# A second DMA queue on ScalarE, shared places for the memory pieces, and refitted engine choices in a two-block transformer kernel

## The chip, the cores and the metric

One core of a Trainium2 chip runs the whole program. The core has a TensorE (PE in the profile, with its weight loads as PEld), a VectorE (DVE), a ScalarE (ACT), a GpSimd (POOL) and a SyncE (SP), each of which takes its own instructions strictly in order, and 16 DMA engines. A transfer is started by an instruction on one of the engines. That instruction waits, like any other, until what it needs is there, and whatever stands behind it on its engine waits with it. The metric is device time in microseconds (us), the median of several runs.

## The reference

All arrays are fp32, with 256 tokens of width 1024. The first block mixes tokens in two ways (block attention over 8 heads, and differential attention over 4 heads, both with a relative position bias), attends to a memory, and ends with a SwiGLU. The second block has an RWKV-7 layer and a latent-attention (MLA) layer with a SwiGLU each. Cut to what matters here:

```python
# first block
h = rms_norm(x, mix_norm_g)
qa, ka, va, qb, kb, vb = split(h @ w_in)
oa = moba_attention(qa, ka, va, rel_bias_table[:, :8])     # logits + bias[bucket(t - s)], softmax
ob = diff_attention(qb, kb, vb, rel_bias_table[:, 8:], lam)
x = x + concat(oa, ob) @ w_out
x = x + memory_cross_attention(x, mem)                     # keys and values from rms_norm(mem)
x = x + (silu(g @ w_gate) * (g @ w_up)) @ w_down           # g = rms_norm(x)
x = rms_norm(x, final_norm_g)
# second block: RWKV-7 layer, whose state S follows, token by token and head by head,
S = S * w[t] + (S @ a[t]) b[t]^T + v[t] k[t]^T ;  y[t] = S @ r[t]
# ... then group norm, a bonus from r * k * r_k, a gate, memory attention, w_out, SwiGLU;
# MLA layer with rope, memory attention, w_out, SwiGLU;
return rms_norm(x, final_norm_g)
```

## The kernel before

Every weight product is done in three passes, since each fp32 operand is split into a high and a low part: `ah` and `al` are the parts of an activation, `wh` and `wl` those of a weight, and `acc` receives `ah*wh + ah*wl + al*wh`. Weights come in panels of 512 KB (two blocks of 128 rows by 512 columns). `panel` loads a panel into `wr` by a DMA issued on SP; there are three such buffers. A CAST on ScalarE or VectorE makes `wh`, and a subtraction on VectorE makes `wl`. TensorE uses them in `gemm`.

Everything is recorded first as a list of operations from many generators, and then put in order for each engine. The class `Order` does this: `link` finds the dependences and `play` runs a list scheduler over them with a table of costs. DMAs have a cost of issuing and of starting (`DMA_ISSUE`, `DMA_START`) and one clock `dma` of the bytes moved; `RUSH` adds an offset to the priority of each kind of operation. `LEAN` shifts which engine takes an operation that several can do, and `SIDE` names operations that go to VectorE instead of the default GpSimd (or the other way round). The result is a fixed order for each engine, found before the program runs. All instructions are emitted from one line (L2730), so a row is told by its tiles.

The places that matter here:

- **Start.** `setup` makes constants, one tiny ScalarE ACTIVATE (`warm`), and a few matmuls on zeros. The gains (all norm vectors in one tile, `gains`) and the input (`xres`, four pieces of 256 KB) are loaded by SP, between the first weight panels.
- **Bias** (`rel_bias`). The bucket table times a one-hot matrix gives a vector, which goes to memory (`relonce`), is copied there into 24 rows (`rel`), and is read back skewed as the tile `bias` (128 x 256 x 12, 1.5 MB, two DMAs). VectorE adds it to the scores (`e<-pst,bias`).
- **Memory** (`project_mem`). The memory's 8 blocks come in four pieces (`memt`); both blocks' memories go through it, the second's under the name `mem_2t`.
- **Inverses** (`inverses`). The RWKV-7 layer is computed in chunks, each with a triangular inverse. Its matrices `m271h` and `m271l` (first half of the tokens; `m272h` and `m272l` the second) go to memory as `d_m`, come back as 96 rows (`kk<-d_m`), and 31 steps of forward substitution run on GpSimd (first half, `kk`, `subtmp`) or VectorE (second half, `tm`). The result goes out as `d_x` and back as `xt<-d_x`. VectorE masks `xt` (`xt<-xt,m`), and TensorE merges blocks of it (`ident,xt`, then `ymerge` and `x` products).
- **Semaphores.** Each DMA counts on one of eight counters (`DMAHW0` to `DMAHW7`), taken in turn in program order over all issuing engines. A DMA also waits for the counter's earlier DMA.

## Time and profile before

| what | value |
|---|---|
| median of 3 runs | 1139.57 us (1138.84 to 1144.2) |
| profiled execution, its own time | 1143.02 us |
| span of the profiled execution | 1141.3 us |
| mean granted TensorE clock | 0.986 |
| busy share PE, DVE, ACT, POOL | 97%, 75%, 38%, 15% |
| DMA | 183.27 MB, mean 161 GB/s |

The busy share is busy time over span. A clock of 1.00 is 2.4 GHz; a stretch at 1.2 GHz shows as 0.50, and matmuls there take longer without TensorE being idle, so the loss of a stretch has two parts: idle time, and busy time at the lower level. The idle time in brackets at the end of a row is what the engine stood still before that row, with the instruction or transfer that ended it.

### The profile page before, as it was taken

To read this page: it belongs to the slowest core of one execution; us is meant where nothing else is said; L and a number is where in the kernel's file an instruction comes from. 1 tells how busy PE (TensorE), PEld (TensorE's weight loads), DVE (VectorE), ACT (ScalarE), POOL (GpSimd) and SP (SyncE) were. 2 spreads that over 40 slices of the span, in tenths; PEclk is the share of its full clock that TensorE was granted. 3 is DMA by queue.
4 is the path that set the end of the run, shared out by engine and by line. 5 is a ranking of instruction groups with operands and counts; after the bars stand their busy time and mean duration, and the time that the engine had idled before them with its cause. 6 is when DMAs were issued, how large, how long until landed. Compare 5 with 4: busy or idle time off the path is not lost.

```text
span 1141.3 us, 21650 instructions
## 1 busy us (share of the span) xinstructions
PE 1110.4 (97%) x8716; PEld 1052.6 (92%) x8716; DVE 854.8 (75%) x1454; ACT 429.5 (38%) x857; POOL 171.3 (15%) x199
## 2 busy tenths in 40 slices
PE   8899999999999999899979999999999999999997
PEld 7798999999999999799768999999999889999985
DVE  7658577677776777979787877766878968777584
ACT  5437442545223214635323532223235765212400
POOL 1200101024111013016601121120012002111100
PEclk9999999999999999899989999999999999999999
DMA  8744355266564655347320355556654425555563
GB/s 260 231 153 145 120 176 181 86 193 208 168 208 140 214 187 180 121 117 215 102 65 14 96 182 180 176 163 186 195 169 140 153 95 170 184 185 179 175 207 105
DMA packets 116164, 183.27 MB, mean 161 GB/s; under 512 B 19175, under 2 KB 41480, under 8 KB 116040
## 3 DMA queue, kind: packets, MB, share of 16 engines
q1 hardware_dynamic: 115920, 181.37, 51.8%
q8 instruction: 68, 1.11, 0.4%
q0 software_dynamic: 144, 0.52, 0.2%
q14 instruction: 32, 0.26, 0.1%
HBM read 178.84 MB, written 3.48 MB: 160 GB/s over the span
## 4 chain that ended last, share of the span: by engine, by line
PE 84%; DVE 8%; DMA 4%; ACT 2%; issue 1%; SPq 0%; POOLq 0%; POOL 0%; ACTq 0%; DVEq 0%
PE acc L2730 73%; PE pst L2730 11%; DVE wl L2730 3%; DMA wr<-in_w_in_dram 1%; DVE e L2730 1%; ACT wh L2730 1%; DMA wr<-in_a_ffn_down_dram 1%; DVE tm L2730 1%; DVE qt L2730 0%; DMA wr<-in_b_w_out_dram 0%; DMA wr<-in_w_down_dram 0%; ACT e L2730 0%; DVE wh L2730 0%; DMA xres<-in_x_t_dram 0%; DMA wr<-in_a_ffn_gu_dram 0%
## 5 line engine op out<-in xcount | busy, mean ns | idle before, releaser
L2730 DVE TENSOR_TENSOR wl<-wr,wh 128x1024 fp32r<-128x1024 f32 (+3 forms) x358 | 411.4, 1157 | 107.5 <-ACT wh L2730 93.9
L2730 PE MATMUL acc<-ah,wh 128*128 128x256 f32 x2224 | 482.9, 283 | 4.6 <-ACT ah L2730 2.3
L2730 PE MATMUL acc<-ah,wl 128*128 128x256 f32 x2224 | 481.4, 284 | 2.0 <-DVE wl L2730 1.7
L2730 PE MATMUL acc<-al,wh 128*128 128x256 f32 x2224 | 481.6, 283 | 0.4 <-DVE al L2730 0.4
L2730 PEld LDWEIGHTS acc<-ah,wh 128*128 128x128 f32 x2224 | 357.9, 189 | 10.1 <-ACT ah L2730 3.6
L2730 PEld LDWEIGHTS acc<-ah,wl 128*128 128x128 f32 x2224 | 357.3, 189 | 5.7 <-DVE wl L2730 3.4
L2730 PEld LDWEIGHTS acc<-al,wh 128*128 128x128 f32 x2224 | 357.6, 189 | 2.7 <-DVE al L2730 1.3
L2730 ACT CAST wh<-wr 128x1024 fp32r<-128x1024 f32 (+4 forms) x199 | 181.3, 915 | 371.0 <-PE acc L2730 284.0
L2730 DVE CAST wh<-wr 128x1024 fp32r<-128x1024 f32 (+2 forms) x159 | 115.2, 726 | 68.1 <-PE acc L2730 46.8
L2730 POOL TENSOR_TENSOR h<-h,bc 128x512 f32<-128x512 f32 x33 | 51.6, 1568 | 267.9 <-ACT h L2730 267.7
L2730 PE MATMUL acc<-wh,ah 128*128 128x512 f32 (+2 forms) x212 | 66.2, 372 | 2.6 <-ACT wh L2730 2.4
L2730 PE MATMUL acc<-wl,ah 128*128 128x512 f32 (+2 forms) x212 | 66.1, 370 | 0.7 <-DVE wl L2730 0.5
L2730 PE MATMUL acc<-wh,al 128*128 128x512 f32 (+2 forms) x212 | 66.7, 373 | 0.0
L2730 POOL TENSOR_TENSOR tm<-tm 128x512 f32<-128x512 f32 (+1 forms) x18 | 27.4, 1525 | 222.3 <-ACT tm L2730 188.3
L2730 PEld LDWEIGHTS acc<-wh,ah 128*128 128x128 f32 x212 | 39.8, 193 | 9.4 <-ACT wh L2730 3.2
L2730 PEld LDWEIGHTS acc<-wl,ah 128*128 128x128 f32 x212 | 39.9, 192 | 7.9 <-DVE wl L2730 1.3
L2730 PEld LDWEIGHTS acc<-wh,al 128*128 128x128 f32 x212 | 39.8, 192 | 7.0 <-issue 0.3
L2730 ACT ACTIVATE h<-h 128x512 f32<-128x512 f32 x33 | 20.4, 629 | 62.3 <-DVE h L2730 62.1
L2730 ACT CAST ah<-h 128x512 fp32r<-128x512 f32 x32 | 19.7, 621 | 39.4 <-DVE h L2730 39.2
L2730 ACT ACTIVATE ah<-xres,gains 128x256 fp32r<-128x256 f32 x55 | 24.9, 500 | 16.4 <-DVE xres L2730 14.9
L2730 DVE TENSOR_TENSOR xres<-acc,xres 128x512 f32<-128x512 f32 x24 | 16.3, 687 | 18.9 <-PE acc L2730 18.8
L2730 DVE SCALAR_TENSOR_TENSOR al<-xres,gains,ah 128x256 fp32r<-128x256 f32 x56 | 28.6, 542 | 1.0 <-ACT ah L2730 0.9
(350 smaller groups left out, 1027.6 us busy)
## 6 DMA issues: line engine op xcount, KB each, us to landing
wr<-in_a_ffn_gu_dram SPq DMA_DIRECT2D x40, 512.0 KB, 3.8
wr<-in_b_ffn_gu_dram SPq DMA_DIRECT2D x40, 512.0 KB, 3.9
wr<-in_w_in_dram SPq DMA_DIRECT2D x22, 512.0 KB, 4.6
wr<-in_w_down_dram SPq DMA_DIRECT2D x22, 512.0 KB, 4.6
wr<-in_a_ffn_down_dram SPq DMA_DIRECT2D x22, 512.0 KB, 4.5
wr<-in_b_ffn_down_dram SPq DMA_DIRECT2D x22, 512.0 KB, 3.8
wr<-in_w_gate_dram SPq DMA_DIRECT2D x20, 512.0 KB, 4.3
wr<-in_w_up_dram SPq DMA_DIRECT2D x20, 512.0 KB, 4.0
```

Source lines behind the costliest of these rows:

```text
L2730: emit(*map(again, x.args), **{k: again(v) for k, v in x.kw.items()})
```

## The change

It does four things. 27 DMAs that SP issued are issued by ScalarE: the gains, the four pieces of the input, the one-hot matrix and the table, `relonce`, `rel` and both parts of `bias`, and all transfers of the inverses. In the planner each issuing engine gets a DMA clock of its own. The pieces of both memories come from one pool under shared names, so that the second memory's pieces take the places of the first's. And the tables that set order and engines (`RUSH`, one entry of `LEAN`, `SIDE`) are new. In `SIDE`, `last` and `sq` are dropped (two additions of the output and of the squares go to GpSimd), and `rls`, `ms` and `rk` are added (the scaling of mean squares and the product of r and k go to VectorE). In `setup`, gains and input are now ahead of the `warm` ACTIVATE.

```diff
-    DMA_ISSUE = {"sync": 450.0, "gpsimd": 1000.0}
-    DMA_START = {"sync": 1100.0, "gpsimd": 1900.0}
+    DMA_ISSUE = {"sync": 450.0, "scalar": 450.0, "gpsimd": 1000.0}
+    DMA_START = {"sync": 1100.0, "scalar": 1100.0, "gpsimd": 1900.0}
...
-        order, dma, table = [], 0.0, None
+        order, dma, table = [], dict.fromkeys(names, 0.0), None
...
-                dma = max(dma, ready[i]) + op.size / 360.0
-                free[e] = end = max(free[e] + self.DMA_ISSUE[e], dma + self.DMA_START[e])
+                dma[e] = max(dma[e], ready[i]) + op.size / 360.0
+                free[e] = end = max(free[e] + self.DMA_ISSUE[e], dma[e] + self.DMA_START[e])
...
-                dma = end = max(dma, start + self.DMA_START[e]) + op.size / (360.0 if start > self.DMA_COLD else 240.0)
+                end = max(dma[e], start + self.DMA_START[e]) + op.size / (360.0 if start > self.DMA_COLD else 240.0)
+                dma[e] = end
...
-RUSH = {'a_k1152.0': 21100, 'a_k768.0': -1000, ...
+RUSH = {'a_k1152.0': 12300, 'a_k768.0': 4400, ...
...
-LEAN = {... 'rope': 3462, ...
-SIDE = {'last': 'vector', 'gate': 'vector', 'kk': 'vector', 'rope': 'vector', 'sq': 'vector', 'x': 'vector'}
+LEAN = {... 'rope': 4671, ...
+SIDE = {'gate': 'vector', 'kk': 'vector', 'rls': 'vector', 'rope': 'vector', 'x': 'vector', 'ms': 'vector', 'rk': 'vector'}
...
+        self.x = cp.tile([128, 8, S], F32, name="xres")
+        self.load_gains()
         nc.scalar.activation(self.small(1, "warm", 1), self.neghalf[:, :1], AF.Square)
...
-        self.x = cp.tile([128, 8, S], F32, name="xres")
-        self.load_gains()
...
-        self.nc.sync.dma_start(gt, self.a["gains"])
+        self.nc.scalar.dma_start(gt, self.a["gains"])
...
+        self.turns.pop("memt", None)
...
-        nc.sync.dma_start(once, vec)
+        nc.scalar.dma_start(once, vec)
...
-        nc.sync.dma_start(rows, once.strided(0, [[0, m], [1, n]]))
+        nc.scalar.dma_start(rows, once.strided(0, [[0, m], [1, n]]))
...
-            nc.sync.dma_start(bias[:, j:j + 128].rearrange("p j h -> p (j h)"),
+            nc.scalar.dma_start(bias[:, j:j + 128].rearrange("p j h -> p (j h)"),
...
-            nc.sync.dma_start(self.x[:, b:b + 2],
+            nc.scalar.dma_start(self.x[:, b:b + 2],
...
-                t2 = self.go(self.later(norm, self.project_mem(pool, "mem", g["mem_norm_g"], memacts, mn, 2)), "mem")
+                t2 = self.go(self.later(norm, self.project_mem(self.memp, "mem", g["mem_norm_g"], memacts, mn, 2)), "mem")
...
-        self.t_mem = self.go(self.project_mem(self.memp, "mem_2", g["mem_norm_g_2"], self.memacts, self.mn, 1), "a_mem")
+        self.t_mem = self.go(self.project_mem(self.memp, "mem_2", g["mem_norm_g_2"], self.memacts, self.mn, 2), "a_mem")
...
-                nc.sync.dma_start(d_m[c][6 * i:6 * i + 6, :128].rearrange("u s t -> s u t"), self.mbs[c, i])
+                nc.scalar.dma_start(d_m[c][6 * i:6 * i + 6, :128].rearrange("u s t -> s u t"), self.mbs[c, i])
...
-                nc.sync.dma_start(ms[48 * i:48 * i + 48], d_m[c].strided(0, [[32 * 128 + 32, 48], [128, 32], [1, 32]]))
-            nc.sync.dma_start(xs, a["sub_start"])
+                nc.scalar.dma_start(ms[48 * i:48 * i + 48], d_m[c].strided(0, [[32 * 128 + 32, 48], [128, 32], [1, 32]]))
+            nc.scalar.dma_start(xs, a["sub_start"])
...
-                nc.sync.dma_start(self.d_x[c].strided(32 * i, [[1024, 48], [64, 16], [1, 32]]), xs[48 * i:48 * i + 48])
+                nc.scalar.dma_start(self.d_x[c].strided(32 * i, [[1024, 48], [64, 16], [1, 32]]), xs[48 * i:48 * i + 48])
...
-            nc.sync.dma_start(last, self.d_x[c].rearrange("u b s t -> (b s) u t"))
+            nc.scalar.dma_start(last, self.d_x[c].rearrange("u b s t -> (b s) u t"))
```

The orders show what this does on each engine. In them a number behind a name tells copies of a tile apart, and the bracket lists the semaphores on which a row waits.

ScalarE before, at the start of the program:

```order
L2730 ACT_TABLE_LOAD
L2730 ACTIVATE warm_92<-neghalf 128x1 [waits Pool_49]
L2730 CAST wh_70<-wr_69 128x512 [waits DMAHW0_49]
L2730 CAST wh_70<-wr_69 128x512 [waits DMAHW1_49]
L2730 CAST wh_73<-wr_72 128x512 [waits DMAHW2_49]
L2730 ACTIVATE ah_81<-xres,gains 128x256 [waits DMAHW4_49,DMAHW3_49]
```

ScalarE now, at the same place (there `DMAHW0` counts the gains, `DMAHW2` the first piece of the input, `DMAHW3` the second half panel of weights):

```order
L2732 DMA gains<-in_gains_dram 128x149
L2732 DMA xres<-in_x_t_dram 128x2x256 x3
L2732 DMA xres<-in_x_t_dram 128x2x256 [waits DMAHW0_49]
L2732 DMA onehot<-in_rel_onehot_dram 33x384 [waits DMAHW2_49]
L2732 DMA reltab<-in_rel_bias_table_dram 32x12 [waits DMAHW3_49,DVE_49]
L2732 ACT_TABLE_LOAD
L2732 ACTIVATE warm_92<-neghalf 128x1 [waits Pool_49]
L2732 CAST wh_70<-wr_69 128x512 [waits DMAHW1_49]
L2732 ACTIVATE ah_81<-xres,gains 128x256
```

The table load, `warm` and the first cast have moved behind seven DMA issues, of which three wait for a transfer; the second and third casts have moved behind the first `ah`.

SP before, around the first half's inverse (`wr` is a panel of `a_w_out`):

```order
L2730 DMA wr_6669<-in_a_w_out_dram 128x2x512 [waits DMAHW4_49,DVE_49]
L2730 DMA d_x_208<-kk 768x1x32 [waits DMAHW5_49,Pool_49]
L2730 DMA d_x_208<-kk 768x1x32 [waits DMAHW6_49]
L2730 DMA wr_6753<-in_a_w_out_dram 128x2x512 [waits DVE_49]
L2730 DMA xt<-d_x_208 128x12x32 [waits DMAHW5_49,DMAHW6_49,DMAHW0_49,PE_49]
```

ScalarE now, at the same work (`ry` are copies of products, `wh` the casts of `a_w_out` panels):

```order
L2732 CAST wh_6594<-wr_6288 128x1024 [waits DMAHW4_49,PE_49]
L2732 COPY ry<-pst_6591 128x256 [waits PE_49]
L2732 COPY ry<-pst_6603 128x256 [waits PE_49]
L2732 COPY ry<-pst_6626 128x256 [waits PE_49]
L2732 DMA d_x_208<-kk 768x1x32 [waits Pool_49]
L2732 DMA d_x_208<-kk 768x1x32 [waits DMAHW5_49]
L2732 COPY ry<-pst_6658 128x256 [waits PE_49]
L2732 CAST wh_6698<-wr_6462 128x1024 [waits DMAHW7_49,DVE_49,PE_49]
L2732 DMA xt<-d_x_208 128x12x32 [waits DMAHW5_49,DMAHW4_49,DMAHW0_49]
```

The three transfers no longer stand between weight panels on SP, but between copies and a cast on ScalarE.

VectorE before, ahead of the first `xt<-xt,m` (`tm` are steps of the second half's substitution, `vtok` scales of the values, `mr` masked products of the chunks):

```order
L2730 TENSOR_TENSOR mr<-pst_6748,masks 128x128
L2730 TENSOR_TENSOR tm_6435<-tm_6421,tm_6435 96x133 [waits DVE_49]
L2730 TENSOR_TENSOR vtok<-vtok,vmean 128x256 [waits PE_49]
L2730 TENSOR_TENSOR tm_6435<-tm_6435 96x7x19 [waits DVE_49]
L2730 TENSOR_TENSOR vtok<-vtok,bonus 128x256 [waits DVE_49]
L2730 TENSOR_TENSOR tm_6435<-tm_6421,tm_6435 96x126 [waits DVE_49]
L2730 TENSOR_TENSOR tm_6435<-tm_6435 96x7x18 [waits DVE_49]
L2730 TENSOR_TENSOR vtok<-vtok,vmean 128x256 [waits PE_49]
L2730 TENSOR_TENSOR tm_6435<-tm_6421,tm_6435 96x136 [waits DVE_49]
L2730 TENSOR_TENSOR vtok<-vtok,bonus 128x256 [waits DVE_49]
L2730 TENSOR_TENSOR tm_6435<-tm_6435 96x8x17 [waits DVE_49]
L2730 TENSOR_TENSOR xt<-xt,m_6458 128x12x96 [waits DMAHW0_49,Pool_49]
```

VectorE now, ahead of the same instruction:

```order
L2732 TENSOR_TENSOR mk_6734<-pst_6711,masks 128x256 [waits PE_49]
L2732 TENSOR_TENSOR tm_6421<-tm_6481,tm_6421 96x133 [waits DVE_49]
L2732 TENSOR_TENSOR mr<-pst_6709,masks 128x128
L2732 TENSOR_TENSOR tm_6421<-tm_6421 96x7x19 [waits DVE_49]
L2732 TENSOR_TENSOR mr<-pst_6711,masks 128x128
L2732 TENSOR_TENSOR xt<-xt,m_6447 128x12x96 [waits DMAHW0_49,Pool_49]
```

The mask of `xt` has moved ahead of four steps of the other half's substitution and of all the `vtok` scales that stood before it.

## Rows read from the trace of the kernel before

**Rows 1.** The page: busy time (share of the span) by engine, and one group's row

```profile
PE 1110.4 (97%) x8716; PEld 1052.6 (92%) x8716; DVE 854.8 (75%) x1454; ACT 429.5 (38%) x857; POOL 171.3 (15%) x199
...
PE 84%; DVE 8%; DMA 4%; ACT 2%; issue 1%; SPq 0%; POOLq 0%; POOL 0%; ACTq 0%; DVEq 0%
...
L2730 DVE TENSOR_TENSOR wl<-wr,wh 128x1024 fp32r<-128x1024 f32 (+3 forms) x358 | 411.4, 1157 | 107.5 <-ACT wh L2730 93.9
```

**Rows 2.** Stretches: length, busy PE PEld DVE ACT POOL, clock, DMA share, GB/s

```profile
20.00:41.00 21.00, 21.00 (x166) 19.92 (x165) 15.58 (x23) 3.28 (x6) 6.33 (x5) 1.00 0.92 253
41.00:50.00 9.00, 6.07 (x19) 4.42 (x19) 7.05 (x14) 6.23 (x14) 1.21 (x2) 0.81 0.59 202
482.00:490.00 8.00, 6.84 (x37) 6.76 (x37) 5.46 (x11) 5.37 (x5) 5.23 (x2) 0.57 0.35 100
575.00:583.20 8.20, 2.74 (x18) 2.36 (x16) 8.16 (x31) 0.74 (x2) 0.00 (x0) 0.68 0.51 136
583.20:590.00 6.80, 6.68 (x44) 6.04 (x45) 5.78 (x20) 1.70 (x5) 0.00 (x0) 0.63 0.01 2
```

**Rows 3.** Timeline of the start: start us, length us, engine, row [idle before it]

```profile
0.79 1.28 ACT L2730 ACT_TABLE_LOAD   x1 [0.79 <-PEq L2784]
...
3.53 1.26 ACT L2730 CAST wh<-wr 128x512 fp32r<-128x512 f32 x2 [1.25 <-DMA wr<-in_w_in_dram]
...
7.15 0.91 ACT L2730 ACTIVATE ah<-xres,gains 128x256 fp32r<-128x256 f32 x2 [1.34 <-DMA xres<-in_x_t_dram]
...
7.71 0.61 PE L2730 MATMUL acc<-ah,wh 128*128 128x256 f32 x2 [1.86 <-ACT ah L2730]
```

**Rows 4.** Timeline of SP, 19 to 46 us

```profile
22.84 0.84 SPq L2730 DMA_DIRECT2D rel<-relonce  x1
...
28.52 1.29 SPq L2730 DMA_DIRECT2D bias<-rel  x2
29.91 3.22 SPq L2730 DMA_DIRECT2D wr<-in_w_in_dram  x2
```

**Rows 5.** Timeline of 38 to 47 us, where TensorE first waits

```profile
41.45 0.59 DVE L2730 CUSTOM_DVE_ANT_0 e<-pst,bias 128x256 f32<-128x256 f32 x1 [3.87 <-DMA bias<-rel]
...
42.47 1.04 ACT L2730 CAST wh<-wr 128x1024 fp32r<-128x1024 f32 x1 [9.94 <-DMA wr<-in_w_in_dram]
...
43.57 0.74 PE L2730 MATMUL acc<-wh,ah 128*128 128x512 f32 x2 [2.40 <-ACT wh L2730]
```

**Rows 6.** The tile `d_m`: time of its DMAs from issue to landing

```profile
DMA to landing us min/median/max: 3.7/4.5/6.4
```

**Rows 7.** Timeline of TensorE, 481 to 491 us

```profile
483.68 1.01 PE L2730 MATMUL pst<-sel,sq 128*128 128x2 f32 x4 [1.16 <-ACT sq L2730]
```

**Rows 8.** Timelines of POOL, SP, VectorE and TensorE around the first half's merge

```profile
561.70 0.23 POOL L2730 TENSOR_TENSOR kk<-kk,subtmp 96x16 f32<-96x16 f32 x1
...
568.29 1.34 SPq L2730 DMA_DIRECT2D d_x<-kk  x2
...
575.62 0.37 SPq L2730 DMA_DIRECT2D xt<-d_x  x1
...
580.75 0.41 DVE L2730 TENSOR_TENSOR vtok<-vtok,bonus 128x256 f32<-128x256 f32 x1
...
581.30 1.35 DVE L2730 TENSOR_TENSOR xt<-xt,m 128x1152 f32<-128x1152 f32 x1
...
576.51 2.56 PE L2730 MATMUL pst<-vtok,mk 128*128 128x64 f32 x16 [1.33 <-DVE mr L2730]
...
583.24 2.18 PE L2730 MATMUL pst<-ident,xt 128*128 128x128 f32 x9 [4.16 <-DVE xt L2730]
```

**Rows 9.** Timeline of VectorE, second half: last substitution step, second mask

```profile
596.63 0.18 DVE L2730 TENSOR_TENSOR tm<-tm 96x16 f32<-96x16 f32 x1
...
607.72 1.35 DVE L2730 TENSOR_TENSOR xt<-xt,m 128x1152 f32<-128x1152 f32 x1
```

**Rows 10.** Timeline of the end of the span

```profile
1134.49 0.72 ACT L2730 ACTIVATE xtok<-xtok,rstdl 128x512 f32<-128x512 f32 x1 [0.85 <-POOL rstdl L2730]
```

More of the change, by code (lines that the diff above doesn't have):

```diff
@@ new lines @@
+LEAN = {'ab0': 2895, 'carry': 137, 'diff_heads': 125, 'expand1': -3988, 'ffn': 1004, 'w_out': -297, 'gate': 3000, 'small': 4209, 'grams1': 1044, 'a_w_out': 168, 'mix_qk': -3000, 'grams0': 161, 'solve1': 808, 'merge1': 1298, 'a_r384': 3000, 'ab1': 6275, 'room': 128, 'mem': 1690, 'w_in': 770, 'cross_kv_w': 61, 'cross': -65, 'expand0': 537, 'down_w': -84, 'norm1': -235, 'a_lora2304': -49, 'rope': 4671, 'first': -431, 'a_mem_out': 1112, 'b_mem_heads': -246, 'a_mem_kv': -519}
+SIDE = {'gate': 'vector', 'kk': 'vector', 'rls': 'vector', 'rope': 'vector', 'x': 'vector', 'ms': 'vector', 'rk': 'vector'}
@@ L1503, in rel_bias @@
         nc.vector.memset(tab, NEG)
-        nc.sync.dma_start(tab[:32], a["rel_bias_table"])
+        nc.scalar.dma_start(tab[:32], a["rel_bias_table"])
         oh = pool.tile([33, 384], F32, name="onehot")
-        nc.sync.dma_start(oh, a["rel_onehot"])
+        nc.scalar.dma_start(oh, a["rel_onehot"])
         yield 0.0
```

3 lines of the change are left out of this document (1 added, 2 removed).

## The prediction

> **What bounds the kernel now.** I read the page first: TensorE is busy 97% of the span, VectorE 75%, and the chain that ended last runs 84% over TensorE and 8% over VectorE [rows 1]. So TensorE's own work sets about 1110 us, the change takes none of it away, and only what stands beside it can move: the time in which TensorE is idle, and the time in which it runs at the lower clock level. The second view is therefore the table of stretches [rows 2], the third the timelines around each of its weak stretches. There are four that the change touches.
>
> - Start: the first real product begins at 7.71, after 1.86 idle, on a ScalarE activation that waited for the input [rows 3].
> - 41 to 50 us: 6.07 busy of 9.00, so 2.93 idle, with a clock of 0.81; 0.19 of 9.00 is another 1.7 if the low level fell on busy time [rows 2]. Up to 4.6 can be had here.
> - 482 to 490 us: one wait of 1.16 on ScalarE's squares [rows 7], and a clock of 0.57 over 6.84 busy, which is 2.9 [rows 2]. Up to 4.1.
> - 575 to 590 us, the first half's merge: two waits, 1.33 and 4.16 [rows 8], and a clock of 0.68 on 2.74 busy and 0.63 on 6.68, together 0.9 + 2.5 = 3.4 [rows 2]. Up to 8.9.
>
> **The start: what it costs.** Before, ScalarE has loaded its table (1.28, from 0.79) and made three half-panel casts before the input lands [rows 3]; all of that is hidden. In the new order the table load and the first cast stand behind seven DMA issues, and the sixth of these waits until the first piece of the input has landed. From that landing to the first product it now takes two issues of about 0.4 (one took 0.37 for `xt` and half of 1.29 for `bias` [rows 4, 8]), the table load 1.28, one cast 0.63 (half of 1.26), and 0.56 from the activation's start to the product (7.15 to 7.71 [rows 3]): 3.3. Before, it was 0.56. Against this the input is earlier: it stood behind three half panels of 256 KB and the gains, about 1.1 MB with itself, and landed by 7.15, while the first half panel had landed by 3.53 [rows 3]. On a queue of its own it shares with the weights, so that about 0.66 MB have moved when it lands; in between by bytes that is 5.3. First product: 8.6 to 8.9, against 7.71. I take +1.2. The ends: input no earlier than 3.53 gives 6.8 (-0.9), no earlier than before, 7.15, gives 10.5 (+2.8).
>
> **The bias and the panels, 22 to 50 us.** Before, both bias DMAs are issued at 28.52 on SP, and the panel behind them (29.91) is there for its cast only at 42.47; VectorE waits for the bias until 41.45, 3.87 us, and TensorE for the panel's cast until 43.57 [rows 4, 5]. With the bias on ScalarE's queue, the panels are no longer behind 1.5 MB in line. The second memory's piece, 256 KB that was loaded early, comes later, which gives 1.0 back at 253 GB/s [rows 2]. In the new order VectorE needs the bias behind one panel more, which is 3.1 of TensorE work (1110.4 over 358 panels [rows 1]). So the panel can be there in time, and the bias may be as late as it was. The start's delay, which the sum has as a term of its own, brings TensorE here that much later and so makes the panel's task easier. I take 3.6 of the 4.6, with 1.0 left as a wait for the bias. The ends are 4.6 and 0.
>
> What speaks against that: at 20 to 41 us the DMA engines are already busy 0.92 of the time at 253 GB/s [rows 2]. The Trainium skill says (DMA: Bandwidth & Descriptors, Issuing engines are not separate DMA queues) that transfers run on the same 16 engines whichever engine issues them, and that several issuers only save the time of issuing. By that rule the split brings nothing here beyond the order of the bytes and the 256 KB, and the term is near 0; the trace's 0.92 is on its side, and it is the second rival.
>
> **ScalarE as an issuer.** Its DMAs now stand between casts. `rel` waits for `relonce`, and `bias` for `rel`: between the issue of `rel` and that of `bias` there were 5.7 us (22.84 to 28.52 [rows 4]), in which ScalarE now does nothing. It is idle there anyway (3.28 busy of 21.00), and VectorE, which gets the casts of these panels, has 5.4 left of 21.00 [rows 2]: 0. At the inverses, `kk<-d_m` waits for `d_m`, 4.5 from issue to landing [rows 6], with one cast between; a panel covers 3.1, so about 1.4 shows, of which casts ahead hide a part: +1.0, with 0 and 1.4 plus a slow stretch of 1.7 as ends.
>
> **The merge.** POOL ends the substitution at 561.70, yet `d_x` is issued at 568.29, 6.6 later, and `xt` comes back by an issue at 575.62, both in line with weight panels on SP [rows 8]. On ScalarE the first stands behind three copies, the second behind one copy and one cast, so that `xt` can be there some 6 us earlier. That alone gives little: from 575 to 583.2 VectorE is busy 8.16 of 8.20 [rows 2], so what TensorE waits for is VectorE's line, not the transfer. But in the new order the mask stands ahead of four substitution steps and four `vtok` scales; a scale and a step take 0.55 together (580.75 to 581.30 [rows 8]), so 2.2, and the deferred products of two chunk groups give about 1.5 more, by the same rate of some 0.3 each. The mask comes 3.7 earlier, and TensorE's 5.5 of waiting shrinks by as much. Of the 3.4 of lost clock I count 1.3. What is late next is the second half: its last step ended at 596.63 and its mask began 11.1 later [rows 9], and the work now put behind the first mask falls before it. VectorE has only 1.0 free in 583 to 590 [rows 2], so I give back 1.0. Net 4.0; the ends are 8.9 gained, and, if all that is saved waits again at the second mask with a slow stretch, 1.7 lost.
>
> **The rest.** In 482 to 490 the squares' small products stand apart in the new order instead of in one bunch: 2.0 of the 4.1, ends 0 and 4.1. At the end of the span a scaling of 0.72 on ScalarE stood ahead of the second tile's squares [rows 10]; they have changed places: 0.7. Engine choices move a few small instructions each way between VectorE and POOL; nothing waits there: 0. Elsewhere a refitted order shifts small waits both ways, with a bound of 3 each way.
>
> **Sum.** +1.2 - 3.6 + 1.0 - 4.0 - 2.0 - 0.7 = -8.1. Against the profiled execution's own time, 1143.02, that is 1134.9; the median of the runs shown is 3.45 lower, so 1139.57 - 8.1 = 1131.5. A difference under 0.5% (5.7 us) is no change that can be told: faster means below 1133.9, slower above 1145.3.
>
> **Rivals.**
> 1. The forecast, 1127 to 1136 with its own terms' ends: 0.45. About 0.33 of it is below 1133.9.
> 2. The engines' bandwidth is what counts at 41 us, and the split gives nothing there: 1131.5 + 3.6 = 1135.1. For it: the 0.92. Against: the order of the bytes does change, in favour of the panel that TensorE waits for. 0.17, of it 0.06 faster.
> 3. The merge's gain waits again in the second half, since VectorE's work is only moved: 1131.5 + 4.0 = 1135.5. For it: 8.16 of 8.20. Against: VectorE has been idle 0.15 and more of the time after 583.2 (5.78 of 6.80). 0.13, of it 0.03 faster.
> 4. ScalarE, held by its own transfers, starves TensorE of casts: slower. It decides once fewer than two panels are cast ahead when ScalarE starts to wait. Then the 5.7 before `bias` shows less one panel of 3.1 (2.6), the 4.5 at `d_m` less one panel (1.4), a few us at `d_x` if POOL is not done (2.0), two of these with a slow stretch of 1.7 each, and the start costs its upper end, 2.8: 12.2. Against it stand the merge's 4.0 and the end's 0.7, while nothing is won at 41 and 482 us: +7.5, 1147.1. For it: the start's chain is of just this kind. Against: ScalarE is busy 38% only. 0.08, of it 0.07 slower.
> 5. Nearly all of the four stretches is won: 4.6 + 4.1 + 8.9 + 0.7 = 18.3, less the start, between 1121 and 1127; 1124. For it: a clock that does not fall once costs nothing afterwards. Against: the merge's VectorE line. 0.17, all faster.
>
> Faster 0.33 + 0.06 + 0.03 + 0.17 = 0.59, slower 0.08 (the 0.07 and some chance of several small losses), same 0.33. The range goes from 1122, inside the fifth case, to 1141, past the second and third with 3 of small waits and 2 to 3 of the spread of the runs; the likeliest case alone is 1127 to 1136.
>
> **What would show it.** Right: the first product at 8.6 to 9 with the table load behind the issues; a wait below 1.5 near 42 us and a clock of 0.9 or more in the 9 us after; `d_x` issued within 2 us of POOL's end and the first mask near 577; a wait before the first `ident,xt` product of 2 or less. Wrong: a wait of 2.4 or more near 42 us that ends with a panel's landing (second case); a new wait of several us before the second `ident,xt` (third); TensorE waiting on casts of ScalarE right behind its DMA issues at 22 to 30, near 520 or near 562 us (fourth). A first product after 10 us, or many new waits of half a us, would make the sum wrong without any of the cases.

## The result, and the profile after

The changed kernel takes 1156.19 us, the median of 4 runs (1155.67 to 1156.88), against 1140.86 before (1138.84 to 1144.2, 4 runs): a ratio of 1.0135, 95% interval 1.012 to 1.0151. It is about 15 us slower where 8 faster were forecast, and above the range of 1122 to 1141. The profiled execution took 1156.88 with a span of 1155.2.

The page of the kernel after first: busy time, the chain, and the two DMA queues (q10 is ScalarE's).

```profile
PE 1117.5 (97%) x8716; PEld 1057.6 (92%) x8716; DVE 864.0 (75%) x1474; ACT 424.1 (37%) x847; POOL 163.0 (14%) x189
...
q1 hardware_dynamic: 98320, 174.62, 50.0%
...
q10 hardware_dynamic: 17600, 6.75, 2.5%
...
PE 82%; DVE 9%; DMA 3%; ACT 3%; issue 2%; ACTq 0%; POOLq 0%; POOL 0%; DVEq 0%
```

Only 6.75 of 183 MB have changed their queue. Shares hardly differ from [rows 1]; nothing here tells of a loss. The table of stretches does (length, busy PE PEld DVE ACT POOL, clock, DMA share, GB/s), after:

```profile
20.00:41.00 21.00, 13.38 (x109) 12.97 (x108) 11.57 (x18) 1.54 (x3) 1.49 (x2) 0.88 0.76 210
30.00:40.00 10.00, 2.97 (x26) 2.76 (x24) 1.43 (x2) 0.91 (x2) 0.00 (x0) 0.80 0.91 225
36.00:47.00 11.00, 6.54 (x33) 6.55 (x34) 6.36 (x10) 2.51 (x5) 1.91 (x3) 0.53 0.72 213
...
469.00:480.00 11.00, 10.40 (x47) 9.75 (x48) 6.52 (x16) 6.09 (x15) 2.27 (x1) 0.53 0.24 68
534.00:542.00 8.00, 8.00 (x47) 7.55 (x47) 4.99 (x11) 2.71 (x10) 6.82 (x16) 0.57 0.58 191
```

and before, in two of them:

```profile
30.00:40.00 10.00, 10.00 (x77) 9.32 (x76) 5.69 (x9) 2.10 (x3) 4.71 (x4) 1.00 1.00 244
36.00:47.00 11.00, 8.07 (x41) 5.99 (x39) 5.34 (x13) 4.23 (x9) 1.01 (x2) 0.93 0.75 216
```

TensorE was busy all of 20 to 41 us before [rows 2]; now it stands still for a third of it. The DMA engines are near full in both kernels at 30 to 40 (1.00 and 0.91). So the DMA engines move about as much (225 and 244 GB/s), but before TensorE still had products to do. A second loss is at 534 to 542, a stretch near 1.2 GHz that before did not have (1.00 from 500 to 540).

Of the 13.9 by which the span of the profiled execution is longer, 6.5 lie in the first stage (up to the end of the last `pst<-ident,rstd` near 460, at 466.09 and before at 459.56) and 6.1 in the RWKV mixing (from there to the end of the last `pst<-st,ar`, 177.05 and before 170.94). The rest makes 1.3.

**Start** (answers [rows 3]; timeline of ScalarE and TensorE: start, length, engine, row, idle before):

```profile
6.51 1.28 ACT L2732 ACT_TABLE_LOAD   x1 [6.51 <-DMA onehot<-in_rel_onehot_dram]
...
7.92 0.60 ACT L2732 CAST wh<-wr 128x512 fp32r<-128x512 f32 x1
...
8.57 0.70 PE L2732 MATMUL acc<-ah,wh 128*128 128x256 f32 x2 [2.34 <-ACT wh L2732]
```

**The stop** (answers [rows 4, 5]; timelines of ScalarE, SP, VectorE and TensorE, 14 to 42 us):

```profile
18.18 1.05 ACT L2732 CAST wh<-wr 128x1024 fp32r<-128x1024 f32 x1 [0.65 <-DVE lampr L2732]
...
24.28 1.31 ACTq L2732 DMA_DIRECT2D bias<-rel  x2
...
21.21 2.71 SPq L2732 DMA_DIRECT2D wr<-in_w_in_dram  x2
24.68 0.37 SPq L2732 DMA_DIRECT2D wr<-in_w_ck_dram  x1
...
38.58 0.69 DVE L2732 CAST wh<-wr 128x1024 fp32r<-128x1024 f32 x1 [8.89 <-DMA wr<-in_w_ck_dram]
...
40.46 0.80 PE L2732 MATMUL acc<-ah,wl 128*128 128x256 f32 x2 [7.49 <-DVE wl L2732]
```

The bias is issued at 24.28, before the panel of `w_ck` at 24.68, which takes 13.8 us to land (38.48 by its landing). Before, that panel and one more were issued ahead of the bias, which came at 28.52 [rows 4].

**`d_m` on ScalarE** (answers [rows 6]; timelines of ScalarE and TensorE, then the time of the DMAs of `d_m` to landing):

```profile
519.04 0.39 ACTq L2732 DMA_DIRECT2D d_m<-m271h  x1
519.93 0.83 ACT L2732 CAST wh<-wr 128x768 fp32r<-128x768 f32 x1 [0.58 <-DMA wr<-in_a_w_in_dram]
523.71 1.66 ACTq L2732 DMA_DIRECT2D kk<-d_m  x2
525.46 0.83 ACT L2732 CAST wh<-wr 128x768 fp32r<-128x768 f32 x1 [4.70 <-DMA wr<-in_a_w_in_dram]
...
528.95 0.39 PE L2732 MATMUL acc<-ah,wl 128*128 128x256 f32 x1 [1.54 <-DVE wl L2732]
...
DMA to landing us min/median/max: 2.8/5.1/6.6
```

For 4.70 from 520.76 ScalarE makes no cast: it waits 2.95 for `d_m`, and the two issues of `kk<-d_m` take 1.66. The cast behind them is late, so `wl` is, and TensorE waits 1.54. The row names the panel's DMA as releaser, but the cast begins 0.1 after the two issues end: it is the issue that held it.

**The merge** (answers [rows 8, 9]; timelines of POOL, ScalarE, TensorE and VectorE):

```profile
570.85 0.23 POOL L2732 TENSOR_TENSOR kk<-kk,subtmp 96x16 f32<-96x16 f32 x1
...
577.64 1.74 ACTq L2732 DMA_DIRECT2D d_x<-kk  x2
...
586.19 1.58 PE L2732 MATMUL pst<-vtok,mk 128*128 128x64 f32 x12 [2.08 <-DVE mr L2732]
...
588.31 1.34 DVE L2732 TENSOR_TENSOR xt<-xt,m 128x1152 f32<-128x1152 f32 x1
...
590.33 1.09 PE L2732 MATMUL pst<-ident,xt 128*128 128x128 f32 x4
...
621.61 0.66 PE L2732 MATMUL pst<-ident,xt 128*128 128x128 f32 x4 [0.91 <-DVE xt L2732]
```

The wait of 4.16 before the first `ident,xt` is gone, as forecast, and the second mask costs 0.91. But the wait for `mr` grew from 1.33 to 2.08, and 589 to 596 us still run at a clock of 0.51. And `d_x` goes out 6.8 after the start of POOL's last step, where SP took 6.6 [rows 8]: the new queue gained nothing there, since its issue stands behind `ry` copies that wait for TensorE.

### The profile page after: what moved, and what is told of

It reads as the page before. It is cut to its first block, busy times and chain, and to the rows that moved or that the text cites. A ratio compares the mean times of both kernels' runs of the same rounds, so it can differ in the third digit from the quotient of the medians.

```text
span 1155.2 us, 21644 instructions
## 1 busy us (share of the span) xinstructions
PE 1117.5 (97%) x8716; PEld 1057.6 (92%) x8716; DVE 864.0 (75%) x1474; ACT 424.1 (37%) x847; POOL 163.0 (14%) x189
## 3 DMA queue, kind: packets, MB, share of 16 engines
q10 hardware_dynamic: 17600, 6.75, 2.5%
## 4 chain that ended last, share of the span: by engine, by line
PE 82%; DVE 9%; DMA 3%; ACT 3%; issue 2%; ACTq 0%; POOLq 0%; POOL 0%; DVEq 0%
PE acc L2732 71%; PE pst L2732 11%; DVE wl L2732 3%; DMA wr<-in_w_ck_dram 1%; ACT wh L2732 1%; DVE tm L2732 1%; DVE e L2732 1%; DVE wh L2732 1%; DMA wr<-in_a_w_in_dram 1%; DVE qt L2732 0%; DMA wr<-in_b_ffn_down_dram 0%; DMA wr<-in_kv_w_up_dram 0%; DMA wr<-in_a_ffn_down_dram 0%; DVE kt L2732 0%; DMA xres<-in_x_t_dram 0%
## 5 line engine op out<-in xcount | busy, mean ns | idle before, releaser
L2732 ACT CAST wh<-wr 128x1024 fp32r<-128x1024 f32 (+4 forms) x192 | 173.8, 911 | 337.5 <-PE acc L2732 280.4
L2732 DVE CAST wh<-wr 128x1024 fp32r<-128x1024 f32 (+2 forms) x166 | 120.0, 725 | 68.3 <-PE acc L2732 42.8
L2732 POOL TENSOR_TENSOR rstd<-rms,neghalf 128x4 f32<-128x4 f32 (+2 forms) x11 | 12.5, 1135 | 145.4 <-DVE rms L2732 145.4
L2732 DVE TENSOR_TENSOR h<-acc,h 128x512 f32<-128x512 f32 x33 | 22.4, 685 | 10.4 <-PE acc L2732 10.4
```

Source lines behind the costliest of these rows:

```text
L2732: emit(*map(again, x.args), **{k: again(v) for k, v in x.kw.items()})
```

## The experiments

Two (a_shared_plan and a_old_tables) are planned anew. The others, but for dma_share, keep the order that the planner found and change it afterwards, at the place where `order = Order(ops).run()` stands; before is 1140.1 to 1141.3 in all of them.

| kernel | made from | median us (range) | ratio to before, 95% |
|---|---|---|---|
| a_bias_sp | after | 1153.86 (1153.22 to 1154.64) | 1.0115, 1.01 to 1.013 |
| a_inv_sp | after | 1148.78 (1147.09 to 1150.18) | 1.0069, 1.0054 to 1.0084 |
| a_all_sp | after | 1151.42 (1149.26 to 1154.56) | 1.0095, 1.0079 to 1.0111 |
| b_all_act | before | 1147.49 (1146.23 to 1149.79) | 1.006, 1.0045 to 1.0074 |
| b_start_act | before | 1143.06 (1140.36 to 1146.79) | 1.002, 1.0008 to 1.0032 |
| b_bias_act | before | 1142.79 (1139.29 to 1144.39) | 1.0018, 1.0004 to 1.0031 |
| b_inv_act | before | 1142.19 (1139.91 to 1145.4) | 1.0016, 1.0004 to 1.0028 |
| a_bias_late | after | 1156.12 (1150.25 to 1159.52) | 1.013, 1.0087 to 1.0174 |
| a_early | after | 1155.31 (1153.49 to 1160.29) | 1.0134, 1.0115 to 1.0152 |
| a_early2 | after | 1152.71 (1149.69 to 1158.19) | 1.0112, 1.0087 to 1.0136 |
| a_fix | after | 1150.07 (1144.49 to 1155.15) | 1.0091, 1.0064 to 1.0118 |
| a_fix_bias | after | 1146.57 (1144.3 to 1149.12) | 1.0055, 1.0041 to 1.0069 |
| a_shared_plan | after | 1174.39 (1171.56 to 1178.66) | 1.0297, 1.0253 to 1.0341 |
| a_old_tables | after | 1158.33 (1155.21 to 1163.69) | 1.016, 1.012 to 1.02 |
| b_merge | before | 1153.3 (1149.56 to 1155.18) | 1.0105, 1.009 to 1.012 |
| b_merge_sp | before | 1146.87 (1146.54 to 1150.91) | 1.0063, 1.005 to 1.0077 |
| b_vtok | before | 1140.52 (1139.24 to 1146.65) | 1.0011, 0.9997 to 1.0025 |

**Which transfers cost.** Groups of them change their engine back, or in the kernel before to ScalarE (`b_...`):

```diff
     order = Order(ops).run()
+    for op in ops:          # a_bias_sp: relonce, rel; a_inv_sp: d_m, d_x, sub_start
+        if op.what == "dma_start" and op.engine == "scalar" and {source, target} & {"relonce", "rel"}:
+            op.engine = "sync"
```

> The changed kernel in its own order, with only the three steps of the bias (relonce, rel, both parts of bias) issued by SP again instead of ScalarE. Theory (the bias, on a queue of its own, takes most of the DMA engines from the weight panel that TensorE needs next; in the changed kernel TensorE stood 7.5 us at 33 us and ran at 1.2 GHz until 47): the 7.5 us stop shrinks to under 3.5 and the time falls by 5 to 8 us from 1156. Rival (the order and the engine of the casts cause the stop, not the queue): the stop stays at 6 us or more, time within 2 us of 1156.

> The changed kernel in its own order, with only the inverses' transfers (d_m, kk, tm, sub_start, d_x, xt) issued by SP again. Theory (ScalarE, held by kk<-d_m from 520.8 to 525.4 us, casts a panel late, TensorE stops 1.5 us at 527 and runs at 1.2 GHz from 535 to 543, together some 5 us): the time falls by 2 to 5 us. Rival (transfers on SP stand behind panels and come later, as before; what is won at 527 is lost at the merge): within 1 us of 1156, or slower.

> The changed kernel in its own order, with all 27 DMAs issued by SP again. If the queue alone made the change slower, the time is that of the kernel before, 1138 to 1143. If the new order and engine choices cost something by themselves, it stays above 1146; the difference to 1140.9 is then the price of the new order (with SP standing in front of panels where the order was not made for it).

> The kernel before in its own order, with the same 27 DMAs issued by ScalarE instead of SP. Theory (the queue is the cost): slower than 1140.9 by 5 us or more, with a stop near 33 to 42 us of over 5. Rival (the new tables are the cost): within 3 us of 1140.9.

> The kernel before with the start's transfers alone (gains, four pieces of the input, one-hot matrix, table) issued by ScalarE; bias and inverses stay on SP. With all 27 on ScalarE the first stage ended 4.3 later and the whole was 6.6 slower. Theory (the start is the greater part of the loss of the first 60 us, since table load and casts stand behind ScalarE's issues and every panel after it is late): 3 to 5 slower than before, 1144 to 1146, with the first product near 9.9. Rival (the bias's transfers on ScalarE's queue are the greater part): 0 to 1.5 slower than before.

> The kernel before with the bias's four transfers alone (relonce, rel, both parts of bias) issued by ScalarE. The start alone cost 2.0, all three groups 6.3 to 6.6. Theory (on a queue of its own the bias's 6-KB pieces overtake the panels, and ScalarE stands still between rel and bias): 2 to 3.5 slower than before, 1143 to 1145, the stop near 41 us longer than 2.40 by 1.5 to 3. Rival (the prediction's: the panel gets ahead of the bias, and the stop shrinks): 1 to 3 faster than before.

> The kernel before with the inverses' transfers alone issued by ScalarE. Taking them off ScalarE in the kernel after gave 7.4. Theory (ScalarE, held in front of kk<-d_m, casts the next panel late; how much this costs depends on what stands behind it in ScalarE's order, which here was not made for it): 1.5 to 4 slower than before, with a new stop near 520 us, and the wait of 4.16 before the first ident,xt unchanged within 1, since VectorE's order sets it. Rival (the prediction's: the transfers leave SP's line, xt comes earlier, and the merge gains): faster than before by 1 to 4, and the wait before ident,xt shrinks to 3 or less.

In the kernel after, the inverses' transfers are worth 7.4 (1156.19 to 1148.78), more than the 2 to 5 of the theory. The bias's are worth 2.3, with intervals that meet, where 5 to 8 were expected; its stop stays as the rival had it (6.56, shown below). In a_inv_sp ScalarE waits for TensorE where it stood still before, and there is no stop (timelines of ScalarE and TensorE):

```profile
519.37 0.84 ACT L2732 CAST wh<-wr 128x768 fp32r<-128x768 f32 x1 [2.26 <-PE acc L2732]
...
523.76 0.83 ACT L2732 CAST wh<-wr 128x768 fp32r<-128x768 f32 x1 [0.77 <-PE acc L2732]
...
578.45 1.94 PE L2732 MATMUL pst<-vtok,mk 128*128 128x64 f32 x12 [2.08 <-DVE mr L2732]
```

The merge's `mr` wait is 2.08 there too and the 4.16 is gone likewise: that gain did not need ScalarE's queue. With all 27 on SP, 10.6 of the loss remain (1.0095). That is the price of the new order together with a line on SP that it was not made for: TensorE waits 3.43 there for the table of the bias, until 12.63. The shared places of the memory pieces are in this kernel too, and no run undoes them alone. From the other side, in the kernel before each group costs 1.8 to 2.3 and all three 6.8 (1.006), so they add up there. Both rivals that saw a gain on that side (bias, inverses) fell. In b_bias_act the stop is 2.55 where it was 2.40, so what the bias costs there does not show at the stop. In b_inv_act two further rows of ScalarE, three scalings and a cast, stand between the issue of `d_m` and that of `kk<-d_m`; no stop appears, against the expected one near 520. What the held engine costs depends on what stands in front of the wait.

**How two queues share the DMA engines.** dma_share is a program of transfers alone: four panels of 512 KB on SP, beside 1.5 MB in two pieces on ScalarE's queue with 6-KB runs (`big`) or 2-KB runs (`mid`), or on SP behind the first panel.

> Transfers alone, no compute; the output is left at zeros. Five phases of four weight panels (512 KB in pieces of 2 KB) on SP's queue: alone; beside two transfers of 768 KB in pieces of 6 KB on ScalarE's queue; beside two of 768 KB in pieces of 2 KB there; with the two of 6-KB pieces on SP's queue behind the first panel; beside four of 192 KB in pieces of 128 bytes on ScalarE's queue. Theory (two queues share the same engines piece by piece, so the queue with longer pieces gets more): all phases move 230 to 400 GB/s in all; the first two panels land about 1.5 times later beside 2-KB pieces than alone, and 2.5 times or more later beside 6-KB pieces. Rival (queues share by bytes): the panels are late by the same factor with 6-KB and with 2-KB pieces. Second rival (queues add up): panels land as early as alone.

Its DMA view (rows: issues, KB each, median to landing):

```profile
big<-in_g_dram ACTq DMA_DIRECT2D x2, 768.0 KB, 6.8
mid<-in_g_dram ACTq DMA_DIRECT2D x2, 768.0 KB, 8.7
big<-in_g_dram SPq DMA_DIRECT2D x2, 768.0 KB, 6.7
```

Alone, the second panel lands 5.4 after the first issue of its phase; beside `mid` on the other queue 7.2, beside `big` 9.0, and with `big` on its own queue ahead of it 9.8. So long runs on a second queue delay this panel nearly as if they stood ahead of it in line. It is 1.33 and 1.67 times as late as alone, less than the theory's 1.5 and 2.5. Both rivals (the same factor for both, and no delay) fall by this one execution. Beside 128-byte runs (a fifth phase, 768 KB in all) the second panel takes 6.7.

In a_bias_sp, where the bias stands behind the `w_ck` panel on SP, the panel lands in 6.4 instead of 13.8, and still the first stage ends no earlier (466.48). The next panel, issued at 28.73 behind the bias, is now the late one, and `ka` stands on VectorE behind its cast:

```profile
41.02 0.69 DVE L2732 CAST wh<-wr 128x1024 fp32r<-128x1024 f32 x1 [6.35 <-DMA wr<-in_w_in_dram]
...
44.42 1.28 DVE L2732 TENSOR_TENSOR ka<-acc,bc 128x512 f32<-128x512 f32 x2
...
45.16 1.65 PE L2732 MATMUL pst<-ka,qa 64*128 64x256 f32 x8 [6.56 <-DVE ka L2732]
```

**The stop of the first stage.** a_bias_late puts the bias on SP behind panel 9. a_early moves ScalarE's `warm` ahead, the issues of the one-hot matrix and the table back, and the cast of panel 3 ahead of the memory's activations; a_early2 does this without touching those issues' place, beyond `warm`.

```diff
+    move(warm, before=first("dma_start", "onehot"))
+    move(first("copy", "wh3", "wr3"), before=first("activation", "ah16", "memt0"))
```

> The changed kernel in its own order, the bias's three steps on SP as in the run before, and both parts of bias moved behind the tenth panel (wr9), where the kernel before has them. Theory (the stop of 6 to 7 us near 40 us comes from the 1.5 MB being sent two panels earlier than before, on whichever queue): the stop shrinks to 2 to 4 us, and the time is 2 to 5 us below the 1153.9 of the run with the bias on SP. Rival (casts and activations stand in a worse order, not the bytes): the stop stays over 6.

> The kernel after with four things moved on ScalarE, none of them to another queue: the warm ACTIVATE with the table load stands behind the input's issues, the issues of the one-hot matrix and of the table behind the third half-panel cast, and the cast of panel 3 ahead of the four ah<-memt and the issue of relonce. Theory (the order of ScalarE's own work at the start, with casts behind issues and behind the memory's activations, makes the first 60 us slow): first product at 7.8 to 8.2 instead of 8.57, panel 3 cast near 15.5 instead of 18.18, panel 6 issued near 18.5 instead of 21.21, the stop before w_ck's product 3 to 5 instead of 7.49, and 3 to 6 faster than after, 1150 to 1153. Rival (the bytes of the bias beside the panels set the stop, not the panels' start): the first product comes earlier but the stop grows by as much; within 1.5 of after.

> The kernel after with two things moved on ScalarE: the warm ACTIVATE with the table load ahead of the issue of the one-hot matrix, and the cast of panel 3 ahead of the four ah<-memt and the issue of relonce. In a_early the one-hot matrix and the table had been put back too, and TensorE waited 4.33 for them at 10.41, which hid what the rest gave. Theory (casts that stand behind issues and behind the memory's activations make panel 6 late, and that makes the stop of 7.49): first product near 8.0 instead of 8.57, panel 3 cast by 15.5 instead of 18.18, the stop 3 to 5, and the first stage ends 3 to 6 earlier than 466.1; 1150 to 1153. Rival (the 1.5 MB of the bias beside the panels set the stop): the two moves give 0.5 at the start and the first stage ends within 1.5 of 466.1; 1154 to 1156.

In a_bias_late the stop only splits, into 0.92 at 38.51 and 4.59 at 42.65, and its 1156.12 is the time of the kernel after: the bias's place in line alone is not the cause. TensorE waits for the scores `e`, and these stand on VectorE behind the `wl` of a late panel:

```profile
45.14 1.23 DVE L2732 TENSOR_TENSOR wl<-wr,wh 128x1024 fp32r<-128x1024 f32 x1 [5.17 <-ACT wh L2732]
46.28 0.37 DVE L2732 CUSTOM_DVE_ANT_0 e<-pst,bias 128x128 f32<-128x128 f32 x1
...
47.24 0.47 PE L2732 MATMUL pst<-ident,e 128*128 128x128 f32 x1 [4.59 <-ACT e L2732]
```

In the kernel before, the panel behind the bias was as slow (issued at 29.91, cast at 42.47 [rows 4, 5]), but VectorE did `ka` and the first `e` (41.45 [rows 5]) ahead of it, and TensorE had their products to do:

```profile
36.30 1.29 DVE L2730 TENSOR_TENSOR ka<-acc,bc 128x512 f32<-128x512 f32 x2 [0.55 <-PE acc L2730]
```

a_early was spoiled by a wait of 4.33 for the one-hot matrix. a_early2 brings the first product to 7.48 and the issue of panel 6 to 19.50, yet the first stage ends at 466.26, after at 466.09 (where `pst<-ident,rstd` ends; before 459.56): the stop moves to 36.36 and is as long. What its profiled run gains lies in the RWKV mixing (170.39 for 177.05); that run is its fastest, and its interval meets that of the kernel after. Its VectorE and TensorE:

```profile
39.66 0.69 DVE L2732 CAST wh<-wr 128x1024 fp32r<-128x1024 f32 x1 [7.23 <-DMA wr<-in_w_in_dram]
...
43.06 1.28 DVE L2732 TENSOR_TENSOR ka<-acc,bc 128x512 f32<-128x512 f32 x2
...
43.79 1.44 PE L2732 MATMUL pst<-ka,qa 64*128 64x256 f32 x6 [7.43 <-DVE ka L2732]
```

`ka` needs only sums that were ready at 36.36, but stands on VectorE behind the cast of a panel that lands at 39.6. a_fix moves it ahead, on top of a_early2, with the inverses on SP; a_fix_bias has the bias on SP too.

```diff
+    for i in reversed(vector[vector.index(first("tensor_copy", "wh9", "wr9")):vector.index(ka[0])]):
+        move(i, behind=ka[1])
```

> The kernel after with three things undone: the inverses' transfers on SP (as a_inv_sp), the two moves on ScalarE of a_early2, and, on VectorE, both ka<-acc,bc ahead of the cast of panel 9 and what followed it. In a_early2 TensorE stopped from 36.36 to 43.75 for ka, whose sums had been there at 36.36: ka stood on VectorE behind the cast of a panel that landed at 39.6. Theory (the stop of the first stage is VectorE's and TensorE's order, made for a plan in which each queue has the full rate, so that the panel was to be there beside the bias): the stop of 7.43 falls to 4 or less in all, the first stage ends at 461 to 464, and the whole takes 1140 to 1145. Rival (the bytes alone: panel and bias are late, whatever the order): TensorE does the scores earlier and then waits as long for the panel, the first stage ends at 465 or later and the whole takes 1145 to 1149.

> As a_fix, with the bias's four transfers on SP too, so that only the start's stay on ScalarE. Theory (a bias on its own queue overtakes the panels): 1 to 3 faster than a_fix. Rival (once it is issued behind two more panels, its queue does not matter): the same as a_fix within 1.

The timelines of a_fix:

```profile
35.97 0.92 PE L2732 MATMUL pst<-ka,qa 64*128 64x256 f32 x8
...
40.54 0.70 PE L2732 MATMUL acc<-wh,ah 128*128 128x512 f32 x2 [2.97 <-DVE wh L2732]
...
39.70 0.69 DVE L2732 CAST wh<-wr 128x1024 fp32r<-128x1024 f32 x1 [3.29 <-DMA wr<-in_w_in_dram]
```

The stop falls from 7.43 to 2.97, with a wait of 0.73 and one of 0.74 behind it, and the first stage ends at 462.78, inside the theory's 461 to 464. The whole took 1150.07, which neither theory nor rival had. Its profiled run took 1144.81 at a mean clock of 0.992, another 1155.15 at 0.984: 0.008 of 1145 is 9 us, so most of this spread can be stretches at the lower level, but in which of them is not seen, as one execution has a trace. a_fix_bias is steadier, with stops of 1.23 and 1.82 and two of 0.7: 3.5 faster than a_fix by the medians, though the intervals meet (1.0055, to 1.0069; 1.0091, from 1.0064). Its first stage ends at 463.19, so there the bias's queue makes no difference any more.

Traces of the kept orders together (one execution each):

| | end of the first stage | RWKV mixing |
|---|---|---|
| order before, transfers of that part on SP | 455.98 to 459.56 (5 traces) | 169.13 to 170.94 (3) |
| order after, bias on ScalarE or SP | 464.98 to 466.48 (6) | |
| a_fix, a_fix_bias | 462.78, 463.19 | 169.55, 168.06 |
| order after, inverses on ScalarE | | 170.39 to 180.24 (5) |
| order after, inverses on SP: a_inv_sp, a_all_sp | 464.98, 467.70 | 169.33, 173.15 |

So differences of 1 or 2 us between single traces tell nothing; that the first stage is slower in the new order, whichever queue has the bias, is clear of them.

**The planner.** a_shared_plan gives it one DMA clock again, a_old_tables the kernel before's `RUSH`, `LEAN` and `SIDE`.

```diff
-                end = max(dma[e], start + self.DMA_START[e]) + ...
+                end = max(dma["sync"], start + self.DMA_START[e]) + ...
```

> The changed kernel, with the planner's one DMA clock for all queues put back, and so planned anew; queues, tables and all else as changed. Theory (the plan that counts each queue's bandwidth as its own sends too much at once): 4 to 10 us below 1156. Rival (the tables were fitted to the other plan and fit this one worse): 1154 to 1165.

> The changed kernel with the tables RUSH, LEAN and SIDE of the kernel before, planned anew; queues and clock per queue as changed. If the new tables are what costs 10 us in the order: 1141 to 1149. If the queues and the clock per queue cost it: 1153 or more.

The first is slower than the kernel after, which neither its theory nor its rival had, the second the same within its interval. The tables fit one plan, and a plan made with others says little of the one edit; these two tell nothing apart.

**The merge.** In the kernel before, b_merge puts the first mask behind the last `mr` and defers 14 substitution steps; b_merge_sp also brings `d_x` and `xt` forward on SP; b_vtok moves the mask past 6 steps and puts 7 `vtok` scales behind the merge.

```diff
+    for i in masks:
+        move(i, behind=last)      # the last mr
+        last = i
```

> The kernel before with one thing moved, on VectorE alone: both instructions of the first mask of xt stand right behind the last mr ahead of them, and the 14 steps of the other half's substitution that stood between them and the last wl are put back behind it, with all later steps one place on. No transfer changes its queue. Theory (the merge's gain comes from VectorE's order, no ScalarE queue is needed): the mask starts at about 578 instead of 581.30, the wait of 4.16 before the first ident,xt shrinks to 2 or less, and as the second half's last step stays near 596 to 598 the gain lasts: 3 to 6 faster than before, 1135 to 1138. Rival 1 (what is saved waits again before the second half's merge): the wait before ident,xt shrinks but one of 2 to 4 appears near 608, the same as before within 1. Rival 2 (the transfer xt<-d_x sets the mask's start, so that SP's queue is the limit): the mask starts at 580 or later and nothing is won.

> As b_merge, and on SP both d_x issues stand ahead of the weight panel that was issued at 567.81, and the issue of xt<-d_x ahead of the panel that was issued at 575.06. Theory: d_x goes out near 562, xt has landed by 573, so the mask begins as soon as VectorE is there, near 577; 0 to 1.5 faster than b_merge, 1134 to 1137. Rival (the transfers matter, VectorE's order alone does little): 3 or more faster than b_merge. Rival 2 (a panel that is issued later is missed by TensorE): a new wait for wh or wl at 575 to 600, slower than b_merge.

> The kernel before with VectorE's order alone changed around the first merge, otherwise than in b_merge: the mask of xt stands right behind the last mr, the 7 vtok scales that stood around it go behind the last copy of the merge (where VectorE was idle 2.94 at 598), and the 6 substitution steps that stood ahead of the mask follow it one by one; the 8 steps between mk and mr, which cost only some 0.19 each there, stay. b_merge had deferred 14 steps, which stood alone (0.32 each) ahead of the copies of ymerge. Theory (the merge's gain lies in what else VectorE does between mr and the copies of ymerge): first ident,xt 2 to 2.7 earlier than 583.24, no wait above 0.5 before the ymerge products, 1.5 to 4 faster than before, 1137.5 to 1140. Rival (VectorE's line is full, what is deferred waits again at ymerge or at the second half's mask): same as before within 1.5, with a new wait of 1 to 2 at 585 or near 605.

A clear miss. VectorE and TensorE in b_merge, and the stretch after it:

```profile
578.09 1.36 DVE L2730 TENSOR_TENSOR xt<-xt,m 128x1152 f32<-128x1152 f32 x1 [2.92 <-DMA xt<-d_x]
...
579.96 2.18 PE L2730 MATMUL pst<-ident,xt 128*128 128x128 f32 x9 [3.99 <-DVE xt L2730]
585.54 0.96 PE L2730 MATMUL pst<-ymerge,xt 128*96 128x64 f32 x8 [2.02 <-DVE ymerge L2730]
...
601.13 1.11 PE L2730 MATMUL pst<-xt,ymerge 128*64 128x64 f32 x8 [2.96 <-ACT ymerge L2730]
...
599.00:611.00 12.00, 9.87 (x53) 9.68 (x53) 4.21 (x15) 3.22 (x10) 1.22 (x2) 0.57 0.34 68
```

The mask is 3.2 earlier, as wanted. But a step that stands alone starts 0.32 after the last, and between other work it had cost about 0.2; so the deferred steps hold VectorE when the copies of `ymerge` are due, TensorE waits there instead, and 12 us near 1.2 GHz follow. b_vtok had a wait of 3.23 for 4.16 and four of 0.4 to 0.65 behind it: the same time as before. b_merge_sp, with `d_x` and `xt` earlier, is 6.4 faster than b_merge by the medians, where 0 to 1.5 were expected, and still slower than before: the transfers matter in this order more than thought. VectorE's line is full, and no run won by deferring on it alone. That the kernel after has no wait of 4.16 because TensorE's products of two chunk groups now stand between the `ident,xt` (590.33, and 591.21 `vtok,mk`) and fill the waits is argued from its rows; no run tested it alone.

## Why the prediction was wrong

- **What bounds it**: right. TensorE's waits and clock moved the time, though not as thought.
- **Start, +1.2**: right. 8.57 against 7.71 is +0.86, for the reason given; in the kernel before the start alone cost 2.2 (1143.06 against 1140.86).
- **Bias and panels, -3.6**: the step that failed, with the largest error. "So the panel can be there in time" did not happen: the panel took 13.8 to landing, TensorE ran dry at 32.97 and stood 7.49 instead of 2.40, and the first stage ends 6.5 later, 0.86 of it from the start: +5.6 instead of -3.6. Two things were wrong in it.
  - "The panels are no longer behind 1.5 MB in line" took the line on SP for what delays a panel. The DMA engines were near full, and a bias that is issued ahead of the panel or beside it delays it on either queue. The prediction had the evidence, 0.92 at 253 GB/s [rows 2], and its own sign of this came: a wait above 2.4 that ends with a panel's landing (second case). The Trainium skill (DMA: Bandwidth & Descriptors, Issuing engines are not separate DMA queues), which it weighed, says that transfers of all issuing engines run on the same 16 DMA engines and interleave, and that issuing on several saves only the time of issuing. The trace agrees (0.91 busy, 13.8 to landing) and goes past it, since the order of the bytes also got worse.
  - It did not look at what VectorE and TensorE have left to do while a panel is on its way. In the new order `ka` and `e` stand behind a panel's work. With the bias on SP the panel took 6.4 and TensorE still stopped 6.56; with the bias behind two panels, as before, 0.92 and 4.59. Only `ka` ahead of the cast, with a_early2's moves, brings the end of the first stage some 2 to 4 forward (a_fix); some 3 to 7 stay there, and no run shows their cause. That the plan came out so because its panels and bias were to arrive side by side (a DMA clock per engine, by the diff) is argued.
- **ScalarE as an issuer, +1.0**: the place and the mechanism were right, the size wrong: 7.4 by a_inv_sp. The 4.5 of waiting less one panel was taken as 1.4; the trace has 1.54. What was left out is what follows: 8 us at 0.57, 3.4 lost. The rest of the 7.4 has no single row. In these traces it is also a threshold. From the issue of `d_m<-m271h` to that of `kk<-d_m` it takes 4.67 in the kernel after, 4.46 in a_bias_sp, 4.94 in a_bias_late and 5.39 in a_early, and TensorE stops 1.54 to 1.63 in all four; in the profiled run of a_early2, with the same order on ScalarE at this place, it takes 3.66 and the stop is 0.38 (ScalarE's timeline):

```profile
519.27 1.34 ACTq L2732 DMA_DIRECT2D kk<-d_m  x2
520.70 0.83 ACT L2732 CAST wh<-wr 128x768 fp32r<-128x768 f32 x1 [3.75 <-PE acc L2732]
```

- **The merge, -4.0**: the wait went as forecast, and without the queue as well, but little of it was won. The wait for `mr` grew by 0.75 and the lost clock did not come back (0.51 from 589 to 596). The whole RWKV mixing, this term and the next together, takes 169.33 in a_inv_sp against 170.94 before: 1.6 at most, which is within the spread of the traces. b_merge and b_vtok moved the mask forward in the kernel before and won nothing. Nor did `d_x` go out sooner behind POOL (6.8 for 6.6; both count from the start of POOL's last step, 561.70 before, which the prediction took for its end).
- **482 us, -2.0**: the wait of 1.16 [rows 7] went, but TensorE runs at 0.53 from 469 to 480 instead (10.40 busy, so 4.9 lost): nothing.
- **End, -0.7**: 0.2 (7.56 to 7.34 behind the last product).

So the fourth rival, priced at 1147.1 with a chance of 0.08, named one half of the loss (ScalarE held at `d_m`), and no case had the other: a first stage that ends later, with the bias ahead of the panels and VectorE's work behind them. The second rival ended at "nothing won". In the kernel after the parts do not simply add: undone one by one they give 7.4, 2.3 and 3.5 (a_early2; the last two with intervals that meet that of the kernel after), but a_all_sp gives only 4.8. Its trace has the wait of 3.43 for the table, which the kernel after does not have, and 173.15 in the RWKV mixing; how much of that is chance no run tells. What stays open is the 6.3 by which a_fix_bias is still slower than before. By its trace that lies in the first stage (463.19 against 455.98 to 459.56); the start's transfers, which cost 2.2 in the kernel before, may be a part of it. No version was faster than the kernel before.

## What to carry to other kernels

Where the DMA engines are near full (0.91 here), a second queue changes the order of the bytes, so ask which tile is now fetched later, how many products TensorE has until then, and which small work on VectorE those products wait for. Before giving an engine's queue to a transfer that waits for another, count what stands between the two issues and what stands behind: here the price was a threshold, and behind a stop of 1.54 came 3.4 in a slow stretch. An order fitted by a planner is one piece: a gain seen at one place of it does not carry over by moving the same instruction elsewhere.

## What the runs showed of the hardware

In the one execution of dma_share, two queues do not share the DMA engines by transfer: the panel that lands 5.4 after its phase's first issue alone takes 7.2 beside 2-KB runs and 9.0 beside 6-KB runs of the same 1.5 MB. The Trainium skill (DMA: Bandwidth & Descriptors, Queues, rings and completion order) says that an engine goes round the queues packet by packet. That fits if longer runs make longer packets, since they then get the larger share, though no run here looked at one engine's packets.
